# Argmax, gather and scatter-add on one core: one one-hot for both lists, a first load in two parts, and the last scatters behind the fallback branch with one-word transfers after them

## The chip, the cores and the metric

One core of a Trainium2 chip. The metric is the device time of one execution in microseconds (us). "Span" is the profiled execution, which is some 2 us shorter than its device time.

## The reference

```python
# scores (8, 2048, 2048) float32, values (8, 2048, 2560) float32, both random normal
best_j = np.argmax(scores, axis=2)                  # (8, 2048)
gathered = values[b_idx, best_j, :].copy()
out = np.zeros_like(values)
np.add.at(out, (b_idx, best_j, slice(None)), gathered)
```

Row j of batch b of the output is values[b, j] times the number of score rows whose maximum stands in column j. So the kernel counts. Rows drawn once are copied, rows drawn never are zeroed, and rows drawn several times are gathered, multiplied by their count and scattered.

## The kernel before

VectorE finds the argmax of 128 rows at a time (MAX8, FIND_INDEX8) and TensorE sums one-hots into counts. For each batch `value_steps` then issues sixteen "copies" of 128 rows with out-of-range indices for the rows that are not meant, and builds two dense lists of row numbers, one of the zero rows and one of the "many" rows. It builds them as a product of a one-hot over 128 places and the row numbers:

```python
        first = (6, NT)[b] if b < 2 else 4            # NT = 16
        for t in range(first):
            copy_once(t)                              # GpSimd: indirect DMA, DRAM to DRAM
        # ... rank of each row in its list, c = 0 zero rows, c = 1 many rows
        yield
        # ... lo = place mod 128, hi = place // 128, for both lists
        oh = ohp.tile([P, 2 * NT, P], FP16)
        nc.vector.tensor_tensor(
            out=oh[:], in0=lo[:].unsqueeze(2).to_broadcast([P, 2 * NT, P]),
            in1=fill_f[:].unsqueeze(1).to_broadcast([P, 2 * NT, P]), op=ALU.is_equal)
        # ... rm, rz: row numbers (and counts) at column hi
        for t in range(NT):
            nc.tensor.matmul(out=m_ps[:], lhsT=oh[:, NT + t, :], rhs=rm[:, t, :, :].rearrange("p a k -> p (a k)"),
                             start=(t == 0), stop=(t == NT - 1))
        for t in range(NT):
            nc.tensor.matmul(out=z_ps[:], lhsT=oh[:, t, :], rhs=rz[:, t, :], start=(t == 0), stop=(t == NT - 1))
        yield
        yield
        # ... lists to zi, mi and counts mc
        if b == 0:
            zeros()                                   # scatters of zero rows, copies in between
            # ... ten yields
            gathers()
        else:
            gathers()                                 # gather, multiply on ScalarE, copies in between
            zeros()
        for k in range(MCAP):                         # MCAP = 5
            scatter(staged[k], mi[:, k:k + 1])
```

A `yield` hands over to the counting of the next batch. The gathers go to six staging slots in turn (`stage()`), so a gather waits for the earlier scatter out of its slot. Batch 0 runs four steps of `value_steps` at once, the others step by step between row tiles of the next batch. The end:

```python
    nc.gpsimd.wait_ge(landed, 16 * n_free[0])         # copies and zero scatters have landed
    more = nc.values_load(over_i[0:1, 0:1], engines=[mybir.EngineType.Pool], min_val=0, max_val=2)
    with tc.If(more > 0):                             # a list was longer than its share; never with these inputs
        # ... the rest of each list, for any input
```

Of the kernel before, what the change touches and what calls it, by code (L numbers as in the profile page):

```python
# [36 lines left out]
def kernel(  # L37
# [117 lines left out]
    vslot = [0]  # L155

    def stage():
        v = vbig[:, vslot[0] * H:(vslot[0] + 1) * H]
        vslot[0] = (vslot[0] + 1) % NV
        return v  # L160

    def count_steps(b, cnt_ps):

        am = None
        for u in range(NT // R):
# [4 lines left out]
            else:  # L170
                s_tile = spool.tile([P, R * S], FP32, name="s_tile")[:]
            nc.sync.dma_start(
                out=s_tile, in_=scores[b, u * R * P:(u + 1) * R * P, :].rearrange("(p r) s -> p (r s)", r=R))
# [29 lines left out]
    def level_engines(rank, lo, hi):  # L203
# [54 lines left out]
        nc.vector.tensor_single_scalar(out=hi, in_=nth[:], scalar=3, op=ALU.logical_shift_right)  # L258
        lane = lev.tile([P, NT], U32)
        nc.vector.tensor_single_scalar(out=lane[:], in_=nth[:], scalar=LE - 1, op=ALU.bitwise_and)  # L260
        nc.vector.scalar_tensor_tensor(out=lo, in0=lane[:], scalar=float(NE), in1=eng[:], op0=ALU.mult, op1=ALU.add)

    def value_steps(b, cnt_ps):
# [17 lines left out]
        first = (6, NT)[b] if b < 2 else 4  # L281
# [25 lines left out]
        place = fin.tile([P, 2, NT], U32)  # L307
        nc.vector.tensor_copy(place[:], rank[:])
        lo = fin.tile([P, 2 * NT], U32)
        nc.vector.tensor_single_scalar(out=lo[:], in_=place[:].rearrange("p c t -> p (c t)"), scalar=P - 1, op=ALU.bitwise_and)  # L310
        hi = fin.tile([P, 2, NT], U32)
        nc.vector.tensor_single_scalar(out=hi[:], in_=place[:], scalar=7, op=ALU.logical_shift_right)
        if b == B - 1:
            level_engines(rank[:, 0, :], lo[:, 0:NT], hi[:, 0, :])
        oh = ohp.tile([P, 2 * NT, P], FP16)
        nc.vector.tensor_tensor(  # L316
            out=oh[:], in0=lo[:].unsqueeze(2).to_broadcast([P, 2 * NT, P]),
            in1=fill_f[:].unsqueeze(1).to_broadcast([P, 2 * NT, P]), op=ALU.is_equal)
# [4 lines left out]
        rz = fin.tile([P, NT, NT], FP16)  # L323
        nc.vector.tensor_tensor(out=rz[:], in0=ez[:], in1=row1_f[:].unsqueeze(2).to_broadcast([P, NT, NT]), op=ALU.mult)  # L324
# [4 lines left out]
        rm = fin.tile([P, NT, 2, NM], FP16)  # L329
        nc.vector.tensor_tensor(out=rm[:, :, 0, :], in0=em[:], in1=row1_f[:].unsqueeze(2).to_broadcast([P, NT, NM]), op=ALU.mult)  # L330
        nc.vector.tensor_tensor(out=rm[:, :, 1, :], in0=em[:], in1=cnt[:].unsqueeze(2).to_broadcast([P, NT, NM]), op=ALU.mult)  # L331
        m_ps = psum_f.tile([P, 2 * NM], FP32)
        z_ps = psum_f.tile([P, NT], FP32)
        for t in range(NT):
            nc.tensor.matmul(out=m_ps[:], lhsT=oh[:, NT + t, :], rhs=rm[:, t, :, :].rearrange("p a k -> p (a k)"),  # L335
                             start=(t == 0), stop=(t == NT - 1))
        for t in range(NT):
            nc.tensor.matmul(out=z_ps[:], lhsT=oh[:, t, :], rhs=rz[:, t, :], start=(t == 0), stop=(t == NT - 1))  # L338
# [6 lines left out]
        for src, dst, n in ((m_ps, mi, NM), (z_ps, zi, NT)):  # L345
            e = fin.tile([P, n], FP32, name=f"empty{n}")
            nc.vector.tensor_scalar(out=e[:], in0=src[:, 0:n], scalar1=0.0, scalar2=BIG, op0=ALU.is_equal, op1=ALU.mult)
            nc.vector.scalar_tensor_tensor(out=dst, in0=e[:], scalar=float(b * S - 1), in1=src[:, 0:n], op0=ALU.add, op1=ALU.add)
        nc.vector.tensor_copy(mc, m_ps[:, NM:2 * NM])
# [13 lines left out]
        def zeros():  # L363
            for k in range(ZLAST if b == B - 1 else ZCAP):
                scatter(zrow[:], zi[:, k:k + 1], free_running)
                if rest:
                    copy_once(rest.pop(0))


        if b == 0:  # L370
            zeros()

            for _ in range(10):
                yield
            gathers()
        else:
            gathers()
            zeros()
        for k in range(MCAP):
            scatter(staged[k], mi[:, k:k + 1])  # L380
# [3 lines left out]
    with tc.manual_schedule(engines={ET.PE, ET.DVE, ET.Activation, ET.SP}):  # L384
        pending = iter(())
        for b in range(B):
            cnt_ps = psum_c.tile([P, NT], FP32)
            for _ in count_steps(b, cnt_ps):
                next(pending, None)
            for _ in pending:  # L390
                pass
            pending = value_steps(b, cnt_ps)
            if b == 0:
                for _ in range(4):
                    next(pending)
# [12 lines left out]
    nc.gpsimd.wait_ge(landed, 16 * n_free[0])  # L408
    more = nc.values_load(over_i[0:1, 0:1], engines=[mybir.EngineType.Pool], min_val=0, max_val=2)
    with tc.If(more > 0):  # L410
        for b in range(B):
            for k in range(ZLAST if b == B - 1 else ZCAP, NT):
                scatter(zrow[:], zero_i[:, b * NT + k:b * NT + k + 1])
            for k in range(MCAP, NM):
                v = stage()
                i = b * NM + k
                gather(v, many_i[:, i:i + 1])
                nc.gpsimd.tensor_scalar(out=v, in0=v, scalar1=many_c[:, i:i + 1], scalar2=None, op0=ALU.mult)
                scatter(v, many_i[:, i:i + 1])

# [29 lines left out]
```

## Time and profile before

| | before |
|---|---|
| device time, median of 3 | 845.58 us |
| span | 843.6 us |
| VectorE busy | 696.7 us (83%) |
| DMA traffic | 347 MB |
| last landing of a scatter | 835.2 us |
| end of the span after it | 8.4 us |

What bounds the kernel is worked out in the prediction. Two lines of before, one from the timeline of VectorE (start, duration, what it waited for) and one from the page's groups of instructions (count, then busy us and mean ns of one, then idle us before them):

```profile
8.81 2.29 DVE L180 MAX8 mx<-vbig 128x8 f32<-128x2048 f32 x1 [6.45 <-DMA vbig<-in_scores_dram]
```

```profile
L316 DVE TENSOR_TENSOR oh<-lo,fill_f 128x4096 f16<-128x4096 uint32 x8 | 35.4, 4426 | 0.0
```

### The profile page before, as it was taken

What the parts mean: (1) busy time and instruction counts of PE and PEld (TensorE: products, weight loads), DVE (VectorE), ACT (ScalarE), POOL (GpSimd) and SP (SyncE); (2) the same over time, 40 slices, a digit from 0 to 9 for tenths busy, and PEclk for the clock granted to TensorE, in tenths of its full rate; (3) what the DMA queues carried; (4) which work ended last, traced back from release to release, by engine and by line L of the source; (5) the groups of instructions that cost most, each with busy time, mean ns of one, the idle gap of its engine ahead of it and who ended that gap; (6) DMA issues with size and microseconds to landing.
All of it is one profiled execution on the core that took longest, in us unless ns stands there. A gap on an engine that the chain in (4) does not pass through costs nothing.

```text
span 843.6 us, 2305 instructions
## 1 busy us (share of the span) xinstructions
PE 18.1 (2%) x401; PEld 17.0 (2%) x401; DVE 696.7 (83%) x793; ACT 103.0 (12%) x43; POOL 286.5 (34%) x277
## 2 busy tenths in 40 slices
PE   0000000000000000000000000000000000000000
PEld 0000000000000000000000000000000000000000
DVE  6999999999999999999999999999999998000000
ACT  2000000500041002210003200022000500500500
POOL 0000643137312163140263400662105725745720
DMA  9999899999999999999999999999999999999992
GB/s 376 430 428 428 308 414 420 426 395 375 426 428 427 426 428 428 426 425 427 431 425 425 428 427 427 424 429 428 426 429 420 426 424 414 422 423 423 424 417 121
DMA packets 47968, 347.05 MB, mean 411 GB/s; under 512 B 18998, under 2 KB 18998, under 8 KB 18998
## 3 DMA queue, kind: packets, MB, share of 16 engines
q0 software_dynamic: 38736, 212.67, 61.1%
q1 hardware_dynamic: 9216, 134.22, 37.6%
q14 instruction: 13, 0.11, 0.0%
q8 instruction: 3, 0.05, 0.0%
HBM read 354.42 MB, written 300.15 MB: 776 GB/s over the span
## 4 chain that ended last, share of the span: by engine, by line
DVE 68%; DMA 9%; POOL 8%; issue 6%; another core or an unknown queue 5%; PE 0%; POOLq 0%
DVE am L181 30%; DVE mx L180 28%; DMA out_dram<-vbig,many_i 8%; DVE oh L316 3%; POOL out_dram L151 3%; POOL out_dram L33 3%; DVE oh_lo L190 2%; POOL vbig L146 1%; DMA vbig<-in_scores_dram 1%; DVE lo L186 1%; DVE oh_hi L194 0%; DVE rz L324 0%; DVE ez L320 0%; DVE hi L188 0%
## 5 line engine op out<-in xcount | busy, mean ns | idle before, releaser
L181 DVE FIND_INDEX8 am<-mx,s_tile 128x8 uint32<-128x2048 f32 x116 | 265.0, 2285 | 0.0
L180 DVE MAX8 mx<-s_tile 128x8 f32<-128x2048 f32 x116 | 264.3, 2279 | 0.0
L33 POOL DMA_INDIRECT out_dram<-in_values_dram,ones_i x128 | 133.9, 1046 | 145.8 <-DVE m L287 107.7
L357 ACT ACTIVATE vbig<-vbig,many_c 128x2560 f32<-128x2560 f32 x40 | 96.8, 2427 | 697.2 <-DMA vbig<-in_values_dram,many_i 697.2
L146 POOL DMA_INDIRECT vbig<-in_values_dram,many_i x40 | 46.8, 1169 | 231.9 <-DMA out_dram<-vbig,many_i 182.1
L151 POOL DMA_INDIRECT out_dram<-vbig,many_i x40 | 44.9, 1122 | 123.1 <-ACT vbig L357 118.6
L151 POOL DMA_INDIRECT out_dram<-zrow,zero_i x61 | 59.8, 981 | 18.9 <-issue 18.3
L316 DVE TENSOR_TENSOR oh<-lo,fill_f 128x4096 f16<-128x4096 uint32 x8 | 35.4, 4426 | 0.0
L180 DVE MAX8 mx<-vbig 128x8 f32<-128x2048 f32 x12 | 27.3, 2278 | 6.5 <-DMA vbig<-in_scores_dram 6.5
L181 DVE FIND_INDEX8 am<-mx,vbig 128x8 uint32<-128x2048 f32 x12 | 27.4, 2285 | 0.0
L190 DVE TENSOR_TENSOR oh_lo<-lo,lane_f 128x512 bf16<-128x512 uint32 x32 | 22.3, 696 | 0.4
L199 PE MATMUL cnt_ps<-oh_hi,oh_lo 128*128 128x16 bf16 x128 | 8.1, 174 | 569.3 <-DVE oh_hi L194 569.3
L199 PEld LDWEIGHTS <-oh_lo 128*128 128x128 bf16 x128 | 8.4, 105 | 569.0 <-DVE oh_lo L190 567.9
L181 DVE MATCH_VALUE_LOAD am<-mx,s_tile 128x8 f32 x116 | 10.7, 92 | 4.0
L186 DVE TENSOR_SCALAR lo<-am 128x4 uint32<-128x4 uint32 x32 | 6.1, 191 | 1.1
L194 DVE TENSOR_TENSOR oh_hi<-hi,lane_f 128x64 bf16<-128x64 uint32 x32 | 6.9, 217 | 0.0
L335 PE MATMUL m_ps<-rm,oh 128*128 128x16 f16 x128 | 4.7, 175 | 88.2 <-DVE rm L331 88.2
L335 PEld LDWEIGHTS <-oh 128*128 128x128 f16 x128 | 4.1, 105 | 90.5 <-DVE rm L331 83.5
L188 DVE TENSOR_SCALAR hi<-am 128x4 uint32<-128x4 uint32 x32 | 5.7, 178 | 0.0
L338 PE MATMUL z_ps<-rz,oh 128*128 128x16 f16 x128 | 4.6, 174 | 0.0
L338 PEld LDWEIGHTS <-oh 128*128 128x128 f16 x128 | 4.0, 104 | 0.0
L324 DVE TENSOR_TENSOR rz<-ez,row_f 128x256 f16<-128x256 f16 x8 | 3.4, 424 | 0.3
(92 smaller groups left out, 65.7 us busy)
## 6 DMA issues: line engine op xcount, KB each, us to landing
s_tile<-in_scores_dram SPq DMA_DIRECT2D x58, 2048.0 KB, 12.0
vbig<-in_scores_dram SPq DMA_DIRECT2D x6, 2048.0 KB, 23.7
out_dram<-in_values_dram,ones_i POOLq DMA_INDIRECT x128, 25.6
out_dram<-zrow,zero_i POOLq DMA_INDIRECT x61, 25.8
vbig<-in_values_dram,many_i POOLq DMA_INDIRECT x40, 33.7
out_dram<-vbig,many_i POOLq DMA_INDIRECT x40, 45.4
```

The costliest lines, as they stand in the source:

```text
L33: return eng.add_instruction(ins)
L146: nc.gpsimd.indirect_dma_start(out=v, out_offset=None, in_=values_flat[:, :], in_offset=bass.IndirectOffsetOnAxis(ap=idx, axis=0), bounds_ ...
L151: note(nc.gpsimd.indirect_dma_start(out=out_flat[:, :], out_offset=bass.IndirectOffsetOnAxis(ap=idx, axis=0), in_=v, in_offset=None, bound ...
L180: nc.vector.max(out=mx[:], in_=rows)
L181: nc.vector.max_index(out=am[:, g, :], in_max=mx[:], in_values=rows)
L186: nc.vector.tensor_single_scalar(out=lo[:], in_=am[:, :, 0], scalar=P - 1, op=ALU.bitwise_and)
L190: nc.vector.tensor_tensor(out=oh_lo[:], in0=lo[:].unsqueeze(2).to_broadcast([P, G, P]), in1=lane_f[:].unsqueeze(1).to_broadcast([P, G, P]) ...
L199: nc.tensor.matmul(out=cnt_ps[:], lhsT=oh_lo[:, g, :], rhs=oh_hi[:, g, :], start=(t == 0), stop=(t == NT - 1))
L316: nc.vector.tensor_tensor(out=oh[:], in0=lo[:].unsqueeze(2).to_broadcast([P, 2 * NT, P]), in1=fill_f[:].unsqueeze(1).to_broadcast([P, 2 * ...
L335: nc.tensor.matmul(out=m_ps[:], lhsT=oh[:, NT + t, :], rhs=rm[:, t, :, :].rearrange("p a k -> p (a k)"), start=(t == 0), stop=(t == NT - 1))
L338: nc.tensor.matmul(out=z_ps[:], lhsT=oh[:, t, :], rhs=rz[:, t, :], start=(t == 0), stop=(t == NT - 1))
L357: nc.scalar.activation(out=v, in_=v, func=mybir.ActivationFunctionType.Copy, bias=0.0, scale=mc[:, k:k + 1])
```

## The change

Four intents. A row is in at most one of the two lists, so one one-hot over 16 x 128 places serves both, with the row numbers of both lists side by side in one right-hand side. The first load comes in two halves, so that VectorE can start on the first. Batch 1 is treated like batch 0: six copies first instead of sixteen, its lists at once. The last five scatters go behind the fallback branch. After each of the first four of them has landed, GpSimd moves one word from SBUF to SBUF.

```diff
+            parts = R if b == u == 0 else 1
+            for r in range(parts):
+                part = slice(r * R * S // parts, (r + 1) * R * S // parts)
+                nc.sync.dma_start(out=s_tile[:, part], in_=rows_in[:, part])
 ... (level_engines cut: same quota arithmetic, now returns one place number)
-        first = (6, NT)[b] if b < 2 else 4
+        first = 6 if b < 2 else 4
 ...
-        oh = ohp.tile([P, 2 * NT, P], FP16)
+        lo = fin.tile([P, NT], U32)
+        nc.vector.tensor_tensor(out=lo[:], in0=rank[:, 0, :], in1=rank[:, 1, :], op=ALU.min)
+        nc.vector.tensor_single_scalar(out=lo[:], in_=lo[:], scalar=P - 1, op=ALU.bitwise_and)
+        oh = ohp.tile([P, NT, P], FP16)
 ... (put: columns of many rows, counts, zero rows)
+        l_ps = psum_f.tile([P, 2 * NM + NT], FP32)
         for t in range(NT):
-            nc.tensor.matmul(out=m_ps[:], lhsT=oh[:, NT + t, :], ...)
-        for t in range(NT):
-            nc.tensor.matmul(out=z_ps[:], lhsT=oh[:, t, :], rhs=rz[:, t, :], ...)
+            nc.tensor.matmul(out=l_ps[:], lhsT=oh[:, t, :], rhs=put[:, t, :], start=(t == 0), stop=(t == NT - 1))
 ...
+        if b == B - 1:
+            last_staged.extend(staged)
+            yield
+            return
         for k in range(MCAP):
             scatter(staged[k], mi[:, k:k + 1])
 ...
-            if b == 0:
+            if b < 2:
                 for _ in range(4):
                     next(pending)
 ...
-    nc.gpsimd.wait_ge(landed, 16 * n_free[0])
     more = nc.values_load(over_i[0:1, 0:1], engines=[mybir.EngineType.Pool], min_val=0, max_val=2)
     with tc.If(more > 0):
 ...
+    word = ctx.enter_context(nc.sbuf_tensor([1, 2 * MCAP], FP32))
+    for k in range(MCAP):
+        i = (B - 1) * NM + k
+        scatter(last_staged[k], many_i[:, i:i + 1])
+    d = None
+    for k in range(MCAP - 1):
+        with tc.issue_after(d.ins) if d else nullcontext():
+            nc.gpsimd.memset(last_staged[k][0:1, 0:1], 0.0)
+        nc.gpsimd.tensor_copy(word[:, 2 * k:2 * k + 1], last_staged[k][0:1, 0:1])
+        d = nc.gpsimd.dma_start(out=word[:, 2 * k + 1:2 * k + 2], in_=word[:, 2 * k:2 * k + 1])
+        d.then_inc(landed, 16)
+        tc.info.no_tile_sem_insts.add(d.ins.name)
+        n_free[0] += 1
+    nc.gpsimd.wait_ge(landed, 16 * n_free[0])
```

The memset overwrites a word of a slot that a scatter reads, so it has to wait until that scatter has landed: that is how the word is tied to the landing.

More of the change, by code (lines that the diff above doesn't have):

```diff
@@ L1 @@
 import copy
-from contextlib import ExitStack
+from contextlib import ExitStack, nullcontext
 import concourse.bass as bass
@@ L155 @@
     vslot = [0]
+    last_staged = []
     def stage():
@@ L171, in count_steps @@
                 s_tile = spool.tile([P, R * S], FP32, name="s_tile")[:]
-            nc.sync.dma_start(
-                out=s_tile, in_=scores[b, u * R * P:(u + 1) * R * P, :].rearrange("(p r) s -> p (r s)", r=R))
+            rows_in = scores[b, u * R * P:(u + 1) * R * P, :].rearrange("(p r) s -> p (r s)", r=R)
+            parts = R if b == u == 0 else 1
+            for r in range(parts):
+                part = slice(r * R * S // parts, (r + 1) * R * S // parts)
+                nc.sync.dma_start(out=s_tile[:, part], in_=rows_in[:, part])
             if u * R % G == 0:
@@ L201, in count_steps, with level_engines @@
                 yield
-    def level_engines(rank, lo, hi):
+    def level_engines(rank):
         X = mybir.AxisListType.X
@@ L257, in level_engines @@
         nc.vector.tensor_tensor(out=nth[:], in0=rank, in1=begin[:], op=ALU.subtract)
-        nc.vector.tensor_single_scalar(out=hi, in_=nth[:], scalar=3, op=ALU.logical_shift_right)
         lane = lev.tile([P, NT], U32)
-        nc.vector.tensor_single_scalar(out=lane[:], in_=nth[:], scalar=LE - 1, op=ALU.bitwise_and)
-        nc.vector.scalar_tensor_tensor(out=lo, in0=lane[:], scalar=float(NE), in1=eng[:], op0=ALU.mult, op1=ALU.add)
+        nc.vector.tensor_scalar(out=lane[:], in0=nth[:], scalar1=LE - 1, scalar2=4, op0=ALU.bitwise_and, op1=ALU.logical_shift_left)
+        nc.vector.tensor_scalar(out=nth[:], in0=nth[:], scalar1=3, scalar2=7, op0=ALU.logical_shift_right, op1=ALU.logical_shift_left)
+        nc.vector.tensor_tensor(out=rank, in0=nth[:], in1=lane[:], op=ALU.add)
+        nc.vector.tensor_tensor(out=rank, in0=rank, in1=eng[:], op=ALU.add)
     def value_steps(b, cnt_ps):
@@ L306, in value_steps @@
             nc.vector.tensor_scalar(out=rank[:, c, :], in0=base[:, c, :], scalar1=off_ps[:, c:c + 1], scalar2=None, op0=ALU.add)
-        place = fin.tile([P, 2, NT], U32)
-        nc.vector.tensor_copy(place[:], rank[:])
-        lo = fin.tile([P, 2 * NT], U32)
-        nc.vector.tensor_single_scalar(out=lo[:], in_=place[:].rearrange("p c t -> p (c t)"), scalar=P - 1, op=ALU.bitwise_and)
+        if b == B - 1:
+            level_engines(rank[:, 0, :])
         hi = fin.tile([P, 2, NT], U32)
-        nc.vector.tensor_single_scalar(out=hi[:], in_=place[:], scalar=7, op=ALU.logical_shift_right)
-        if b == B - 1:
-            level_engines(rank[:, 0, :], lo[:, 0:NT], hi[:, 0, :])
-        oh = ohp.tile([P, 2 * NT, P], FP16)
+        nc.vector.tensor_copy(hi[:], rank[:])
+        nc.vector.tensor_single_scalar(out=hi[:], in_=hi[:], scalar=7, op=ALU.logical_shift_right)
+        lo = fin.tile([P, NT], U32)
+        nc.vector.tensor_tensor(out=lo[:], in0=rank[:, 0, :], in1=rank[:, 1, :], op=ALU.min)
+        nc.vector.tensor_single_scalar(out=lo[:], in_=lo[:], scalar=P - 1, op=ALU.bitwise_and)
+        oh = ohp.tile([P, NT, P], FP16)
         nc.vector.tensor_tensor(
-            out=oh[:], in0=lo[:].unsqueeze(2).to_broadcast([P, 2 * NT, P]),
-            in1=fill_f[:].unsqueeze(1).to_broadcast([P, 2 * NT, P]), op=ALU.is_equal)
+            out=oh[:], in0=lo[:].unsqueeze(2).to_broadcast([P, NT, P]),
+            in1=fill_f[:].unsqueeze(1).to_broadcast([P, NT, P]), op=ALU.is_equal)
         ez = fin.tile([P, NT, NT], FP16)
@@ L322, in value_steps @@
             in1=lane_f[:, 0:NT].unsqueeze(1).to_broadcast([P, NT, NT]), op=ALU.is_equal)
-        rz = fin.tile([P, NT, NT], FP16)
-        nc.vector.tensor_tensor(out=rz[:], in0=ez[:], in1=row1_f[:].unsqueeze(2).to_broadcast([P, NT, NT]), op=ALU.mult)
         em = fin.tile([P, NT, NM], FP16)
@@ L328, in value_steps @@
             in1=lane_f[:, 0:NM].unsqueeze(1).to_broadcast([P, NT, NM]), op=ALU.is_equal)
-        rm = fin.tile([P, NT, 2, NM], FP16)
-        nc.vector.tensor_tensor(out=rm[:, :, 0, :], in0=em[:], in1=row1_f[:].unsqueeze(2).to_broadcast([P, NT, NM]), op=ALU.mult)
-        nc.vector.tensor_tensor(out=rm[:, :, 1, :], in0=em[:], in1=cnt[:].unsqueeze(2).to_broadcast([P, NT, NM]), op=ALU.mult)
-        m_ps = psum_f.tile([P, 2 * NM], FP32)
-        z_ps = psum_f.tile([P, NT], FP32)
+        put = fin.tile([P, NT, 2 * NM + NT], FP16)
+        nc.vector.tensor_tensor(out=put[:, :, 0:NM], in0=em[:], in1=row1_f[:].unsqueeze(2).to_broadcast([P, NT, NM]), op=ALU.mult)
+        nc.vector.tensor_tensor(out=put[:, :, NM:2 * NM], in0=em[:], in1=cnt[:].unsqueeze(2).to_broadcast([P, NT, NM]), op=ALU.mult)
+        nc.vector.tensor_tensor(out=put[:, :, 2 * NM:], in0=ez[:], in1=row1_f[:].unsqueeze(2).to_broadcast([P, NT, NT]), op=ALU.mult)
+        l_ps = psum_f.tile([P, 2 * NM + NT], FP32)
         for t in range(NT):
-            nc.tensor.matmul(out=m_ps[:], lhsT=oh[:, NT + t, :], rhs=rm[:, t, :, :].rearrange("p a k -> p (a k)"),
-                             start=(t == 0), stop=(t == NT - 1))
-        for t in range(NT):
-            nc.tensor.matmul(out=z_ps[:], lhsT=oh[:, t, :], rhs=rz[:, t, :], start=(t == 0), stop=(t == NT - 1))
+            nc.tensor.matmul(out=l_ps[:], lhsT=oh[:, t, :], rhs=put[:, t, :], start=(t == 0), stop=(t == NT - 1))
         yield
@@ L344, in value_steps @@
         zi = zero_i[:, b * NT:(b + 1) * NT]
-        for src, dst, n in ((m_ps, mi, NM), (z_ps, zi, NT)):
-            e = fin.tile([P, n], FP32, name=f"empty{n}")
-            nc.vector.tensor_scalar(out=e[:], in0=src[:, 0:n], scalar1=0.0, scalar2=BIG, op0=ALU.is_equal, op1=ALU.mult)
-            nc.vector.scalar_tensor_tensor(out=dst, in0=e[:], scalar=float(b * S - 1), in1=src[:, 0:n], op0=ALU.add, op1=ALU.add)
-        nc.vector.tensor_copy(mc, m_ps[:, NM:2 * NM])
+        e = fin.tile([P, 2 * NM + NT], FP32)
+        nc.vector.tensor_scalar(out=e[:], in0=l_ps[:], scalar1=0.0, scalar2=BIG, op0=ALU.is_equal, op1=ALU.mult)
+        for dst, x, n in ((zi, 2 * NM, NT), (mi, 0, NM)):
+            nc.vector.scalar_tensor_tensor(out=dst, in0=e[:, x:x + n], scalar=float(b * S - 1), in1=l_ps[:, x:x + n],
+                                           op0=ALU.add, op1=ALU.add)
+        nc.vector.tensor_copy(mc, l_ps[:, NM:2 * NM])
         rest = list(range(first, NT))
@@ L378, in value_steps @@
             zeros()
+        if b == B - 1:
+            last_staged.extend(staged)
+            yield
+            return
         for k in range(MCAP):
@@ L406 @@
         nc.vector.tensor_reduce(out=over_i[:], in_=over[:], op=ALU.max, axis=mybir.AxisListType.X)
-    nc.gpsimd.wait_ge(landed, 16 * n_free[0])
     more = nc.values_load(over_i[0:1, 0:1], engines=[mybir.EngineType.Pool], min_val=0, max_val=2)
     with tc.If(more > 0):
+        v = stage()
         for b in range(B):
@@ L414 @@
             for k in range(MCAP, NM):
-                v = stage()
                 i = b * NM + k
```

## The prediction

> **What bounds the kernel now.** I read the page first, its slices before its shares:
>
> ```profile
> DVE  6999999999999999999999999999999998000000
> DMA  9999899999999999999999999999999999999992
> GB/s 376 430 428 428 308 414 420 426 395 375 426 428 427 426 428 428 426 425 427 431 425 425 428 427 427 424 429 428 426 429 420 426 424 414 422 423 423 424 417 121
> ```
>
> VectorE is busy 83% of the span, and the chain that ended last is mostly its MAX8 and FIND_INDEX8. But it has nothing left to do after 716 us of 843.6, while the DMA engines stay full for 105 us more. So the kernel is bound by its 347 MB of traffic: at the rate of the good slices (429 GB/s) they take 809 us, and some 35 us of the span are stretches in which the DMA engines were short of work. A saving counts only where it fills such a stretch. I looked for them with the view that sums stretches of time (the last two columns are the DMA share and GB/s):
>
> ```profile
> 1.00:4.00 3.00, 0.00 (x0) 0.00 (x0) 1.36 (x13) 2.99 (x2) 0.78 (x3) 1.00 0.74 191
> 4.00:84.00 80.00, 0.77 (x12) 0.79 (x12) 74.57 (x61) 3.01 (x2) 0.00 (x0) 1.00 1.01 429
> 84.00:112.00 28.00, 1.45 (x38) 1.40 (x38) 26.37 (x44) 0.00 (x0) 19.06 (x16) 1.00 0.91 334
> 94.00:98.00 4.00, 1.00 (x32) 1.01 (x32) 3.13 (x12) 0.00 (x0) 3.08 (x4) 1.00 0.66 192
> 180.00:214.00 34.00, 1.49 (x38) 1.33 (x38) 33.42 (x48) 0.00 (x0) 26.47 (x23) 1.00 0.98 373
> 214.00:640.00 426.00, 11.25 (x250) 10.54 (x250) 420.52 (x460) 48.45 (x20) 123.41 (x117) 1.00 1.01 427
> 640.00:820.00 180.00, 2.18 (x47) 1.88 (x47) 72.99 (x112) 36.20 (x15) 99.35 (x98) 1.00 1.02 422
> 820.00:836.00 16.00, 0.00 (x0) 0.00 (x0) 0.00 (x0) 0.00 (x0) 0.00 (x0) 1.00 0.53 224
> 836.00:843.60 7.60, 0.00 (x0) 0.00 (x0) 0.00 (x0) 0.00 (x0) 0.00 (x0) 1.00 0.00 0
> ```
>
> Loss of a stretch = length x (1 - rate/429): the first list stage (84 to 112) 28 x (1 - 334/429) = 6.2 us; the second (180 to 214) 34 x (1 - 373/429) = 4.4; 214 to 640 2.0; 640 to 820 2.9; the ragged finish of the 16 DMA engines (820 to 836) 7.6; an empty end of 7.6. The start loses about 2.7. What happens in the first list stage stands in the timeline of GpSimd:
>
> ```profile
> 88.16 1.11 POOL L33 DMA_INDIRECT out_dram<-in_values_dram,ones_i  x1 [86.38 <-DVE m L287]
> 89.57 0.99 POOL L33 DMA_INDIRECT out_dram<-in_values_dram,ones_i  x1 [0.30 <-issue]
> 90.87 4.22 POOL L33 DMA_INDIRECT out_dram<-in_values_dram,ones_i  x1 [0.30 <-issue]
> 95.39 1.02 POOL L33 DMA_INDIRECT out_dram<-in_values_dram,ones_i  x1 [0.30 <-issue]
> ```
>
> An issue takes 1.28 us from start to start, but the third took 4.22 us and the fourth could start only at 95.4: VectorE ran the 128x4096 one-hot of line 316 from 89.8 to 94.2. By then the ten load buffers were full and waiting for VectorE, so there was nothing else to move. A copy moves only rows drawn exactly once, about 37% (1/e) of 128 rows of 10 KB, 0.48 MB; at one per 1.28 us that is 376 GB/s, under what the engines carry. The second list stage has the same illness: sixteen copies in a row (180.8 to 205.8), with one issue of 5.2 us under the one-hot. In the later batches a copy alternates with a fuller transfer and the rate is 427. The end, by its instructions (start times last):
>
> ```profile
> L445 POOLq DRAIN  x3: 40/107/6121, 836.7 to 843.4; - x3
> L410 POOLq INC_SWDGE_SEM  x1: 1340/1340/1340, 835.3 to 835.3; - x1
> ```
>
> After the last scatter's landing (835.2) GpSimd spends 1.34 us [...] where the branch's two ways join, then 6.12 us in a DRAIN, then 0.8 us remain. The branch itself (from 822.5, resuming at 826.3) already hides behind the scatters' landings.
>
> **What the Trainium skill says.** "SBUF — State Buffer", section "SBUF: two separate sides", says a VectorE operation with two SBUF inputs locks GpSimd out, if that reads SBUF, for the whole instruction, and that descriptors of GpSimd's DMAs then can't be written. The trace agrees: 4.22 us instead of 1, ending 0.9 us after the one-hot. "DMA: Bandwidth & Descriptors", section "Issuing engines are not separate DMA queues", says all issuers share the 16 engines; the steady 427 to 429 GB/s with loads and scatters mixed agrees. Its section "Anatomy of one DMA — SWDGE (gpsimd) path" gives a small transfer about 2 us; no one-word transfer is in this trace. "Runtime: NRT & Kernel Launch", section "Instruction fetch mechanics", says a taken branch out of the prefetched window stalls on a fetch: here 2.9 us between the compare (823.4) and the next instruction (826.3). I found no page on what GpSimd's 6.12 us DRAIN consists of.
>
> **The change, part by part.**
>
> *First load in two parts.* VectorE's first MAX8 waits until 8.81 us for the whole 2.1 MB. By the rows above 0.57 MB have moved by 4 us, so 2.1 MB are through at 4 + 1.53/0.429 = 7.6 us, and the landing and wait add 1.2. The first half (1.05 MB) is through at 5.1, so the start is near 6.3 us, 2.4 us earlier. VectorE takes 4.6 us a row tile and a megabyte takes 2.4 us to arrive: it never starves again, and all of batch 0 moves 2.4 us earlier. The DMA engines are saturated with loads meanwhile, so this is worth only what it fills after 84 us.
>
> *One one-hot.* 4096 becomes 2048 columns. From 512 (696 ns) and 4096 (4426 ns) the slope is 1.041 ns a column, so 2.29 us instead of 4.42, and the dense list of batch 0 is 10.1 - 2.1 - about 0.1 = 7.9 us; sixteen matmuls instead of 32 (some 2.8 us less in all on TensorE) lie beside other work. Over eight batches VectorE saves 17 us, nearly all off the path. What counts is that GpSimd is held 2.1 us less.
>
> *First list stage after both.* Copies start at 85.8 instead of 88.2; the load that was missing at 86 to 88 is issued in time; the 18 loads last until about 90.7; the third copy is through at about 90.5, not 95.1; the first zero scatter starts near 95 instead of 99.3. Adding 1.1 us a copy to the loads gives work to about 97, when zero scatters (about 108 rows, 2.6 us each) have come in. Of 6.2 us lost I expect 1.2 to stay: gain 5.0.
>
> *Batch 1 like the others.* Six copies first, the list at once, then copies alternating with gathers and zero scatters. The copy-only stretch shrinks from 25 to about 9 us, but the list now stops the counting for 8 us and so frees no load buffer. Of 4.4 us I keep 2.0: gain 2.4. The shorter one-hots of the other batches: 0.3 (the rate is already 427).
>
> *The end.* The join and its 1.34 us go ahead of the scatters. There they delay the last scatters from 801 to about 806, while the engines have older work until about 820 (five scatters, 1.1 MB each, 13 us, before the first engines run dry at 821): free. I read the one-word transfers as a way to let GpSimd tidy up after landed DMAs piece by piece, under the last scatter, instead of in the DRAIN. Estimate: DRAIN 6.1 to 2.5 us, saving 3.6; the last one-word transfer, started at the fourth scatter's landing, 0.8 us ahead of the fifth's, costs some 2 us after it. With the 1.34: gain 3.0. The ragged finish stays.
>
> Sum: 5.0 + 2.4 + 0.3 + 3.0 = 10.7. I shade it to 10, since losses tend to reappear: 845.6 - 10 = 835.6 us.
>
> **Rivals.** (a) The DRAIN is a fixed cost or is not touched by the small transfers. For it: nothing in the trace varies it. Then the end is 2 us of waiting less 1.34: a loss of 0.7 instead of a gain of 3.0, and 839.5 us. (b) Only the fifth scatter's loose end: the DRAIN falls to about 1 us and both early stages fill entirely: 831. (c) The dense list of batch 1 opens a new gap, no buffer freed for 8 us with GpSimd issuing small copies: the second stage loses 5 us instead of 4.4, and 840. Against it: the load buffer released by the early part of the list (line 306) comes sooner than now. (d) VectorE is the bound, as the chain suggests: then its 17 + 2.4 us would come off, and 826. Against it: the DMA engines at 1.01 to 1.02 from 214 to 820 and the 128 us between VectorE's last work and the end. (e) The branch's fetch meets full DMA engines and the scatters come too late for the engines that finish first; these are not the last ones, and the slack is 9 us: under 1 us.
>
> **Range and chances.** (a) and (c) together make 843 and (b) 831; neither extreme is likely, so 831 to 841. Faster by 2% means under 828.7: it would need all of both stages, the whole DRAIN and part of the ragged finish. I give that 3%. Slower by 2% has no mechanism that I see: 1%.
>
> **What would show it.** First MAX8 at about 6.3 us; line of the one-hot 8 x 2.3 us; no issue of GpSimd over 3 us at 85 to 97; GB/s of 84 to 112 above 410, and of 180 to 214 above 400; the rate from 214 to 820 unchanged; INC_SWDGE_SEM near 805; the DRAIN well below 6 us, with 5 to 6 us from the last scatter's landing to the end. It is wrong if the DRAIN stays at 6, if the dips move to other times instead of closing, or if the ragged finish grows by what the earlier stages gain.

## The result, and the profile after

| | before | after |
|---|---|---|
| device time, median of 6 | 845.49 us | 840.34 us |
| range | 845.15 to 847.15 | 840.14 to 841.88 |
| span | 843.6 | 839.0 |
| VectorE busy | 696.7 | 679.2 |
| last landing of a scatter | 835.2 | 830.1 |
| end of the span after it | 8.4 | 8.9 |

The ratio is 0.994 (95% interval 0.9927 to 0.9953): the same within 2%. A ratio is the mean time of one kernel's fast runs over that of the other's of the same rounds, so it is not quite the ratio of the medians. The gain is 5.2 us (4.6 in the two profiled executions) and not the 10 predicted. All of it lies ahead of the last landing, and behind it half a microsecond was lost.

The slices of the page after, to be read against those in the prediction:

```profile
GB/s 383 427 429 428 381 411 424 425 407 425 424 428 429 425 428 431 425 427 427 428 427 429 428 425 427 427 430 426 426 426 408 417 424 409 414 423 418 424 417 108
```

The two early dips are shallower (the fifth slice 381 instead of 308, the ninth and tenth 407 and 425 instead of 395 and 375). But from the 31st slice on there are dips: the 31st, 32nd, 34th and 35th slices have 408, 417, 409 and 414 where before had 420, 426, 414 and 422. The same in sums of stretches of the kernel after (last column GB/s):

```profile
84.00:112.00 28.00, 1.03 (x22) 0.97 (x22) 26.42 (x45) 0.00 (x0) 20.29 (x19) 1.00 1.00 389
170.00:204.00 34.00, 1.31 (x26) 1.23 (x26) 32.32 (x54) 2.43 (x1) 24.38 (x23) 1.00 1.01 413
204.00:620.00 416.00, 8.86 (x166) 8.54 (x166) 410.54 (x454) 46.02 (x19) 117.15 (x115) 1.00 1.01 427
620.00:805.00 185.00, 1.99 (x35) 1.79 (x35) 74.95 (x122) 36.19 (x15) 96.28 (x98) 1.00 1.01 417
```

and the late stretch of the kernel before:

```profile
620.00:805.00 185.00, 3.45 (x83) 3.07 (x83) 92.68 (x140) 36.20 (x15) 98.48 (x97) 1.00 1.01 422
```

With the prediction's measure (length x (1 - rate/429)) the first list stage loses 2.6 us instead of 6.2, and the second 1.3 instead of 4.4. The late stretch loses 185 x (1 - 417/429) = 5.2 instead of 3.0. So 2.2 us come back there of what was won early. That is an upper figure: 1 GB/s is 0.4 us here, and the control below, the same kernel again, has 419 GB/s there, which gives back 1.3 us.

The parts one by one. The first MAX8 and the one-hot of the kernel after, in the timeline and the groups:

```profile
6.07 2.29 DVE L185 MAX8 mx<-vbig 128x8 f32<-128x2048 f32 x1 [5.00 <-DMA vbig<-in_scores_dram]
```

```profile
L322 DVE TENSOR_TENSOR oh<-lo,fill_f 128x2048 f16<-128x2048 uint32 x8 | 18.3, 2292 | 0.3
```

VectorE starts 2.7 us earlier, and one one-hot takes 2292 ns instead of 4426. The timeline of GpSimd in the first list stage:

```profile
86.22 1.18 POOL L33 DMA_INDIRECT out_dram<-in_values_dram,ones_i  x1 [84.48 <-DVE m L293]
...
89.00 2.36 POOL L33 DMA_INDIRECT out_dram<-in_values_dram,ones_i  x1 [0.31 <-issue]
91.67 1.10 POOL L33 DMA_INDIRECT out_dram<-in_values_dram,ones_i  x1 [0.30 <-issue]
...
95.62 1.00 POOL L151 DMA_INDIRECT out_dram<-zrow,zero_i  x1 [0.30 <-issue]
```

The issue that falls under the one-hot takes 2.36 us (4.22 before), and the first zero scatter goes out at 95.6 (99.3 before). The one-hot and the start are as predicted. The third copy is through at 91.4 (expected 90.5), and the rate from 84 to 112 is 389 GB/s, under the 410 expected. Now the end, first GpSimd's work in its timeline, for the last of the four one-word rounds:

```profile
829.43 0.09 POOL L435 MEMSET vbig<- 1x1 f32 x1 [1.92 <-DMA out_dram<-vbig,many_i]
...
830.05 0.50 POOL L437 DMA_DIRECT2D word<-word  x1 [0.29 <-POOL word L436]
```

then its sequencer's instructions, by line (durations min/median/max in ns, then first and last start in us):

```profile
L467 POOLq DRAIN  x3: 46/102/6447, 831.8 to 838.7; - x3
```

```profile
L416 POOLq COMPARE_BRANCH  x1: 53/53/53, 782.4 to 782.4; - x1
L416 POOLq INC_SWDGE_SEM  x1: 1208/1208/1208, 795.2 to 795.2; - x1
```

The fallback branch and its join are indeed out of the way: the compare is at 782.4 and the join's 1.21 us at 795.2. The first of the last scatters goes out at 797.6, 1.4 us behind the last zero scatter (one issue normally follows another after 1.3). But the DRAIN is as long as ever: 6.45 us (6.12 before). It starts at 831.8, 1.7 us after the last scatter has landed at 830.1, because the wait ahead of it covers the last word as well. Of the four words the fastest landed 1.5 us after its issue, the slowest 4.5 (from the view of the tile `word`):

```profile
DMA to landing us min/median/max: 1.5/4.1/4.5
```

### The profile page after: what moved, and what is told of

The parts are those of the page before. It is cut to its first block, busy times and chain, and to the rows that moved or that the text cites. A ratio compares the mean times of both kernels' runs of the same rounds, so it can differ in the third digit from the quotient of the medians.

```text
span 839.0 us, 2067 instructions
## 1 busy us (share of the span) xinstructions
PE 14.7 (2%) x273; PEld 14.1 (2%) x273; DVE 679.2 (81%) x794; ACT 103.0 (12%) x43; POOL 276.7 (33%) x289
## 4 chain that ended last, share of the span: by engine, by line
DVE 69%; DMA 16%; POOL 5%; issue 4%; another core or an unknown queue 4%; ACT 0%; PE 0%; POOLq 0%; DVEq 0%
DVE am L186 32%; DVE mx L185 29%; DMA out_dram<-vbig,many_i 12%; DMA vbig<-in_values_dram,many_i 3%; DVE oh_lo L195 2%; POOL out_dram L33 2%; POOL out_dram L151 2%; DVE oh L322 2%; POOL vbig L146 1%; DMA vbig<-in_scores_dram 1%; DVE lo L191 1%; DVE oh_hi L199 0%; ACT vbig L360 0%; DVE put L337 0%
## 5 line engine op out<-in xcount | busy, mean ns | idle before, releaser
L33 POOL DMA_INDIRECT out_dram<-in_values_dram,ones_i x128 | 131.4, 1027 | 157.5 <-DVE m L293 119.4
L146 POOL DMA_INDIRECT vbig<-in_values_dram,many_i x40 | 42.4, 1061 | 231.8 <-DMA out_dram<-vbig,many_i 185.1
L151 POOL DMA_INDIRECT out_dram<-vbig,many_i x40 | 38.9, 972 | 121.5 <-ACT vbig L360 117.9
L322 DVE TENSOR_TENSOR oh<-lo,fill_f 128x2048 f16<-128x2048 uint32 x8 | 18.3, 2292 | 0.3
L186 DVE MATCH_VALUE_LOAD am<-mx,s_tile 128x8 f32 x116 | 10.7, 92 | 4.0
L340 PE MATMUL l_ps<-put,oh 128*128 128x32 f16 x128 | 4.7, 188 | 68.9 <-DVE put L337 68.9
L340 PEld LDWEIGHTS <-oh 128*128 128x128 f16 x128 | 4.7, 104 | 70.0 <-DVE oh L322 59.6
L327 DVE TENSOR_TENSOR ez<-hi,lane_f 128x256 f16<-128x256 uint32 x8 | 3.4, 419 | 0.0
L337 DVE TENSOR_TENSOR put<-ez,row_f 128x256 f16<-128x256 f16 x8 | 3.3, 417 | 0.0
```

What stands on the lines that cost most here:

```text
L33: return eng.add_instruction(ins)
L146: nc.gpsimd.indirect_dma_start(out=v, out_offset=None, in_=values_flat[:, :], in_offset=bass.IndirectOffsetOnAxis(ap=idx, axis=0), bounds_ ...
L151: note(nc.gpsimd.indirect_dma_start(out=out_flat[:, :], out_offset=bass.IndirectOffsetOnAxis(ap=idx, axis=0), in_=v, in_offset=None, bound ...
L186: nc.vector.max_index(out=am[:, g, :], in_max=mx[:], in_values=rows)
L322: nc.vector.tensor_tensor(out=oh[:], in0=lo[:].unsqueeze(2).to_broadcast([P, NT, P]), in1=fill_f[:].unsqueeze(1).to_broadcast([P, NT, P]), ...
L340: nc.tensor.matmul(out=l_ps[:], lhsT=oh[:, t, :], rhs=put[:, t, :], start=(t == 0), stop=(t == NT - 1))
```

## The experiments

Twelve runs on three chips, each beside runs of the kernel before on the same chip (medians 846.85, 847.54 and 847.29 us). All were correct. First the tail, then the early parts.

### The tail: which part of it costs what

**No one-word transfers.** The expectations name theories by letter. A: the DRAIN can run beside transfers under way, and the words only delay it. B: the DRAIN is a fixed 6 us behind the last landing, words or none. C: the words do shorten it.

```diff
-    d = None
-    for k in range(MCAP - 1):
-        ... (memset, copy, one-word transfer: all cut)
     nc.gpsimd.wait_ge(landed, 16 * n_free[0])
```

> The changed kernel without the one-word transfers and the memsets and copies before them; the last wait is then for the free-running copies and zero scatters alone. What the DRAIN of 6.1 us (before) and 6.4 us (after) consists of is open. Theory A, fixed work that needs nothing landed: GpSimd reaches the DRAIN at about 817 us, when the free-running transfers have landed, it is over by 824 and the end comes 0.8 us after the last scatter's landing near 830: span 831, time 832.5. Theory B, fixed work that starts only when everything has landed: DRAIN ends near 836.5, span 837.5, time 839. Theory C, work for each transfer that GpSimd has not tidied up after, which the one-word transfers shorten: the DRAIN ends later than 838, span 840 or more, time 841.5 or more.

Measured 835.33 us (834.72 to 836.56), ratio 0.9874. GpSimd's DRAIN, by line:

```profile
L458 POOLq DRAIN  x3: 40/107/15647, 816.5 to 832.7; - x3
```

It starts at 816.5, as soon as the last copies and zero scatters have landed, and ends at 832.1. The last scatter landed at 829.0. So it lies under the landings of the last scatters, except for 3.1 us, and the span ends 3.9 us after the last landing instead of 8.9. B and C fall. A had the direction, but was 2.8 us too hopeful: a part of the DRAIN stays.

**The waits of the words without the words.** The memsets remain, so GpSimd still waits for each landing.

```diff
-        ... (copy and one-word transfer cut)
+    for k in range(MCAP):
+        nc.gpsimd.memset(last_staged[k][0:1, 0:1], 0.0)
     nc.gpsimd.wait_ge(landed, 16 * n_free[0])
```

> The changed kernel with a one-word memset after each of the five last scatters' landings (so GpSimd waits for all five, as in the kernel before) but no copies and no one-word transfers. Theories A and B (the DRAIN is fixed work): it starts near 830.4 us instead of 831.75, lasts 6.1 to 6.4 us, and the span is 837.5, the time 839.0, 1.3 us under the changed kernel. Theory C (the one-word transfers tidy up): the DRAIN is longer than 7 us and the time is 840.5 or more.

Measured 838.60 us (838.10 to 839.35), ratio 0.9908. Its last memset (timeline) and its DRAIN (by line):

```profile
829.94 0.09 POOL L433 MEMSET vbig<- 1x1 f32 x1 [0.69 <-DMA out_dram<-vbig,many_i]
```

```profile
L460 POOLq DRAIN  x3: 40/113/6249, 829.9 to 836.7; - x3
```

With the last landing at 829.9 the DRAIN starts at 829.9 and takes 6.25 us again. This splits the price of the words, as the time from the last landing to the end of the span: 3.9 us with no wait, 7.1 with the waits alone, 8.9 with the words. Arriving late at the DRAIN costs 3.2, and the last word's own landing 1.8.

**Still earlier.** If starting the DRAIN before the last landing hides half of it, would starting it before anything has landed hide the rest? The final wait goes to SyncE.

```diff
     ... (e1: no words)
-    nc.gpsimd.wait_ge(landed, 16 * n_free[0])
+    nc.sync.wait_ge(landed, 16 * n_free[0])
```

> The run without one-word transfers, with the last wait (for copies and zero scatters) on the sync engine, so that GpSimd reaches its DRAIN at about 803 us instead of 816. There the DRAIN began at 816.5, took 15.6 us and ended 3.1 us after the last landing; when all had landed before it, it took 6.1 to 6.4. If the DRAIN is work that goes on beside the landings and only its last part is exposed: it ends about 3 us after the last landing again, and the time is the same 835.3 within 0.5. If an earlier start hides more: 832.5 to 834.

Measured 835.58 us (835.40 to 836.40), ratio 0.9859.

```profile
L458 POOLq DRAIN  x3: 40/113/34033, 799.7 to 834.3; - x3
```

The DRAIN begins right after the last issue and lasts 34 us, but it still ends 3.1 us after the last landing (830.7), and the span 3.9 us after it. So some 3 us follow the last landing however early it starts.

**The control and the best version, on one chip.** The kernel after against itself unchanged, and e1 again.

> The changed kernel itself again, as the control on the same chip for the three beside it. Last landing near 830 us, the end 8.9 us later (DRAIN 6.45 us, begun 1.6 us after the last landing), about 5 us faster than the kernel before in the same rounds.

> The kernel without one-word transfers again, now on one chip with the control. If the one-word transfers cost what the traces say (end 3.9 us after the last landing instead of 8.9): 5.0 us under the control, within 0.7. If the earlier comparison was one of chips: less than 3 us under it.

Measured 840.83 us (840.33 to 841.25), ratio 0.9921, for the kernel after: 6.5 us under the kernel before on that chip, where about 5 were expected. Without the words 835.09 us (834.45 to 836.95), ratio 0.9861: 5.7 us less, just outside the 5.0 within 0.7 that was expected, and 12.2 less than the kernel before on that chip (847.29). In the profiles the stretch behind the last landing is 5.0 us shorter, and the landing itself came 1.1 us earlier (828.8 against 829.9). The DRAINs, of the control and of the version without words:

```profile
L467 POOLq DRAIN  x3: 46/102/6447, 831.5 to 838.4; - x3
```

```profile
L458 POOLq DRAIN  x3: 40/107/15657, 816.2 to 832.4; - x3
```

This version beats both kernels.

**The tail alone, on the kernel before.** All early parts undone, the last scatters behind the branch, no words.

```diff
     ... (kernel before, up to here)
+        if b == B - 1:
+            last_staged.extend(staged)
+            yield
+            return
 ...
-    nc.gpsimd.wait_ge(landed, 16 * n_free[0])
     ... (values_load, branch)
+    for k in range(MCAP):
+        i = (B - 1) * NM + k
+        scatter(last_staged[k], many_i[:, i:i + 1])
+    nc.gpsimd.wait_ge(landed, 16 * n_free[0])
```

> The kernel before with only this of the change: the last scatters follow the branch, the wait for copies and zero scatters comes last, no one-word transfers. If the end is worth what the traces say and independent of the early stages: last landing as in the kernel before (835.2, at most 1 us apart), the DRAIN begun before it and over 3 us after it, time 4.5 us under the kernel before. If moving the scatters behind the branch starves the DMA engines: last landing 2 us or more later. Had the one-word transfers or the early stages been needed for the gain at the end: within 1 us of the kernel before.

Measured 842.37 us (841.63 to 843.69), ratio 0.9943: 4.9 us under the kernel before. Its DRAIN and its stretches:

```profile
L453 POOLq DRAIN  x3: 40/107/15679, 823.3 to 839.6; - x3
```

```profile
84.00:112.00 28.00, 1.45 (x38) 1.40 (x38) 24.36 (x43) 0.00 (x0) 18.87 (x16) 1.00 0.92 338
165.00:215.00 50.00, 1.75 (x42) 1.59 (x42) 49.22 (x62) 2.43 (x1) 27.63 (x24) 1.00 0.98 384
620.00:805.00 185.00, 3.44 (x83) 3.06 (x83) 95.05 (x142) 36.20 (x15) 97.55 (x96) 1.00 1.01 423
```

The last landing is at 836.0, where before's profile has it at 835.2, and the end 3.9 us behind it instead of 8.4. The tail without words is thus worth 4.5 to 4.9 us by itself. Against this run the control shows the early parts by themselves: the last landing comes at 829.9 instead of 836.0, 6.1 us earlier (5.1 between the first two profiles).

### The early parts

**Each part undone**, with the rest of the change, words and all, in place. First the split load:

```diff
-            parts = R if b == u == 0 else 1
+            parts = 1
```

> The changed kernel with the first load in one piece again. The first MAX8 goes from 6.1 back to about 8.8 us; the counts of batch 0 were ready only 2.0 us earlier with the split (85.1 against 87.1), since constants of 0.8 us moved behind the first MAX8. Theory M (a hole in the mean DMA rate is time lost): copies start 2.0 us later and the hole of batch 0 grows by about 1.9 us; time 842.2. Theory S (only the DMA engine that lands last counts): the same here, since that hole stops all 16 engines alike; last landing 1.5 to 2 us later. If neither holds, no change: 840.3.

Measured 842.26 us (842.14 to 842.92), ratio 0.9941. Both theories had 842.2. The first MAX8 is back at 8.62, the first copy goes out at 87.99, the first list stage loses 28 x (1 - 365/429) = 4.2 us instead of 2.6:

```profile
84.00:112.00 28.00, 1.04 (x22) 0.98 (x22) 26.03 (x46) 0.00 (x0) 18.84 (x18) 1.00 0.95 365
```

**Batch 1 as before:**

```diff
-        first = 6 if b < 2 else 4
+        first = (6, NT)[b] if b < 2 else 4
 ...
-            if b < 2:
+            if b == 0:
                 for _ in range(4):
```

> The changed kernel with batch 1 as before (its 16 copies in a row, its list spread over the counting of batch 2). Theory M: the second stage loses 3.0 us more of mean DMA rate, so the time is 843.3. Theory S: in the changed kernel the last landing of batch 1's scatters came only 4.3 us earlier than before, of which 3.6 were there already at batch 0's, so the slowest engine gained about 0.8 us in this stage, and the time is 841.1; the spread between first and last landing after 280 us falls from 30 to about 20 us, as before the change, and the dips after 620 us close.

Measured 842.98 us (841.35 to 843.39), ratio 0.9941.

```profile
165.00:215.00 50.00, 1.31 (x26) 1.24 (x26) 49.20 (x65) 0.87 (x1) 29.61 (x29) 1.00 1.00 392
620.00:805.00 185.00, 2.00 (x35) 1.80 (x35) 74.03 (x122) 36.20 (x15) 95.40 (x97) 1.00 1.01 419
```

The second stage loses 50 x (1 - 392/429) = 4.3 us, against 1.2 in the kernel after over the same stretch (419 GB/s). The late stretch doesn't recover: 4.3. The spread that theory S in the expectation names (the time between the first and the last of the 16 engines' landings of one transfer) was 31 us for the fourth gather of batch 2 and not 20: that detail of S failed, and the time lies by M's 843.3 and not by S's 841.1.

**The one-hot issued twice,** which gives VectorE its old work back, and more:

```diff
         nc.vector.tensor_tensor(out=oh[:], ..., op=ALU.is_equal)
+        nc.vector.tensor_tensor(out=oh[:], ..., op=ALU.is_equal)      # the same again
```

> The changed kernel with the one-hot of 2048 columns computed twice, so that VectorE holds GpSimd and the list takes as long as with two lists. If holding GpSimd in the first two batches is what the halved one-hot was worth: an issue of over 4 us near 88 to 92, the first zero scatter of batch 0 2.2 us later, and a time of 841.8 to 842.5. If VectorE's work itself counted, eight times 2.29 us, it would be 858. If the hole of batch 0 was closed by the split load alone: 840.3.

Measured 843.48 us (840.79 to 843.65), ratio 0.9944.

```profile
84.00:112.00 28.00, 1.04 (x22) 0.98 (x22) 26.10 (x44) 0.00 (x0) 20.37 (x18) 1.00 0.97 372
165.00:215.00 50.00, 1.31 (x26) 1.24 (x26) 47.81 (x63) 6.29 (x4) 32.32 (x30) 1.00 1.00 407
```

The first stage loses 3.7 us, the second 2.6. Parts of the expectation failed: instead of one issue over 4 us there were two, of 2.37 and 2.02 us, the first zero scatter came 1.0 us later (96.66) and not 2.2, and the time is above the range. The eight extra one-hots are 18 us of VectorE, and the loads end at 634.4 instead of 619.3, but the time rises by under 3 us. VectorE's work as such doesn't count; only where it holds up GpSimd and the lists.

By medians the three cost 1.4, 2.2 and 2.7 us against the control's 840.83. That comparison crosses chips. The kernel without words speaks for it, since its medians agree within 0.5 us on all three chips (835.33; 835.58 with the wait on SyncE; 835.09). Against it, the ratios to before (0.9941, 0.9941 and 0.9944) differ by only 0.002 from the control's 0.9921, with intervals that overlap, and hardly at all from the 0.9940 of the first result. So each part may be worth some 1 to 3 us by itself, but that is not shown beyond noise, and their order isn't settled. What is shown is the three together, 6.1 us on the last landing.

**Are the loads the filler that the late stretch lacks?** In the kernel after VectorE gets through the scores sooner, so the loads end at 619.3 (634.9 before), just where the late dips begin. One theory (G in the text) was that the later waits used to be filled by these loads. An idle MAX8 in the lists of batches 2 to 7 slows VectorE, without touching the early stages:

```diff
+        if b >= 2:
+            idle = small.tile([P, 8], FP32, name="idle")
+            nc.vector.max(out=idle[:], in_=zrow[:, 0:S])
```

> The changed kernel with one useless MAX8 over 2048 columns (2.28 us, one input) in the list of batches 2 to 7, which gives VectorE back the 2.1 us a batch that the halved one-hot saved there, without holding GpSimd. Theory G (given back): the loads end 12 us earlier than in the kernel before, and then nothing fills the DMA engines while GpSimd waits for a staging slot; slower lists move the end of the loads from 620 to about 632 us, the dips near 635 to 655 and 695 to 720 us close, and the time falls by 1.5 to 2.5 us to about 838.3 in spite of 14 us more work on VectorE. Rival H (the dips come from engines that hold unequal numbers of rows, whenever the loads end): no change, 840.3 within 0.5. Rival V (VectorE matters at the end): slower, 842 or more.

Measured 840.57 us (839.89 to 841.83), ratio 0.9928. The loads ended at 629.7, and the late stretch stayed as it was:

```profile
620.00:805.00 185.00, 2.57 (x51) 2.36 (x51) 88.94 (x135) 36.20 (x15) 98.61 (x98) 1.00 1.01 416
```

G falls. The time is the one that H named, but its reason, unequal numbers of rows, was not tested. The run also shows that 14 us more work on VectorE cost nothing.

**Zero scatters ahead of the gathers** in batches 5 and 6, to have work queued when a gather has to wait for its slot:

```diff
         if b == 0: ...
+        elif b in (5, 6):
+            zeros()
+            gathers()
         else: ...
```

> The changed kernel with the zero scatters of batches 5 and 6 ahead of their gathers, as batch 0 has it: these need no staging slot, so GpSimd puts seven more transfers (7.7 MB, 18 us) in the queue before it waits for the scatters of the batch before. Theory G: the dips after 620 us shrink to half or less, time about 838.5. Rival H: no change, 840.3 within 0.5. A loss (over 841) would say that the gathers, now later, hold up their own scatters.

Measured 852.96 us (852.61 to 854.11), ratio 1.0083, worse than both kernels.

```profile
640.00:700.00 60.00, 1.74 (x31) 1.53 (x31) 55.97 (x104) 12.14 (x5) 11.09 (x13) 1.00 0.93 384
```

The gathers go out later and so hold up their own scatters: GpSimd sat idle from 645.6 to 680.3, waiting for ScalarE's multiplications, with nothing left to issue.

**A run that told nothing of its question.** The two halves of the load let 0.8 us of VectorE's constants slip in between the first MAX8 and its FIND_INDEX8 and later ones. I tried to put them ahead by fixing their order:

```diff
     ... (e1: no words)
+    with tc.manual_schedule(engines={mybir.EngineType.DVE}):
         row_f = consts.tile([P, NT], FP32)
         ... (all constants of VectorE, unchanged)
```

> The kernel without one-word transfers, and with VectorE's constants (0.8 us) kept ahead of the first MAX8, where it only waits, instead of behind it, where the split load's earlier landing let them slip. The counts of batch 0 should be ready near 84.3 instead of 85.1 us. If the hole of batch 0 still follows VectorE: 0.5 to 0.8 us faster than the run without one-word transfers. If the slowest DMA engine gains nothing more there: the same within 0.4.

Measured 835.50 us (835.23 to 836.57), ratio 0.9862. The timeline shows that the edit didn't do what was meant, since the first constant still follows the first MAX8:

```profile
8.17 0.16 DVE L90 CAST row_f<-row_i 128x16 f32<-128x16 int32 x1
```

So it is one more repeat of e1 and says nothing of the constants. A seventh staging slot was also tried for the late dips, but it didn't fit in SBUF, so there is no run of it.

### The late dips, from the landing records

Before trusting the stretches further I counted, for single transfers, when the first and the last of the 16 DMA engines reported their share (times in us, from the trace's landing records):

| transfer | before: first, last (spread) | after: first, last (spread) |
|---|---|---|
| batch 0, fifth scatter | 177.5, 190.0 (12.5) | 173.6, 186.4 (12.8) |
| batch 1, fifth scatter | 292.7, 310.2 (17.5) | 283.4, 305.8 (22.4) |
| batch 2, fourth gather | 329.2, 354.1 (24.9) | 316.9, 353.7 (36.9) |
| a gather issued at 591.4 / 596.3 | 642.0, 656.5 (14.5) | 632.5, 652.3 (19.8) |

The early filling gave the fastest engine 9.3 us at batch 1's fifth scatter and the slowest only 4.4: the mean rate rises by more than the slowest engine gains. What a larger spread does stands in GpSimd's timeline after, where a gather waits for the scatter out of its slot, and in the stretches around it:

```profile
598.05 0.99 POOL L33 DMA_INDIRECT out_dram<-in_values_dram,ones_i  x1 [0.30 <-issue]
634.83 1.01 POOL L146 DMA_INDIRECT vbig<-in_values_dram,many_i  x1 [35.79 <-DMA out_dram<-vbig,many_i]
```

```profile
630.00:635.00 5.00, 0.00 (x0) 0.00 (x0) 4.93 (x6) 0.00 (x0) 0.17 (x1) 1.00 0.98 406
635.00:640.00 5.00, 0.00 (x0) 0.00 (x0) 4.96 (x4) 0.00 (x0) 3.65 (x4) 1.00 0.94 369
```

A slot is free when the last engine is through with it, here at 634.0. The first engine had landed its share of the gather of 596.3 at 632.5, and behind that only its share of one copy (598.05) was left. The new gather went out at 634.8, 2.3 us after that landing. Before, the wait ended at 639.2, 2.9 us ahead of the first engine's landing at 642.0. Over the runs the rate follows that lead:

| run | next gather issued ahead of the first engine's landing | GB/s from 630 to 640 |
|---|---|---|
| tail alone on before | 3.6 us | 421 |
| before | 2.9 | 422 |
| one-hot twice | 2.2 | 420 |
| batch 1 as before | 0.5 | 414 |
| idle MAX8 | -0.2 | 405 |
| control | -2.2 | 395 |
| after | -2.3 | 387 |

The other six runs with this order of issues have leads of -1.1 to -2.5 and 394 to 403 GB/s. Thirteen profiles show this relation, but no run moved the lead alone, so that the lead is the cause is argued and not shown. This dip is about 0.8 us of the 2.2 that came back: 10 x (422 - 387)/429. The rest lies in smaller dips near 650, 700 and 715. Which early part makes them stays open: the late loss is in every variant with any of the early parts (3.9 to 5.6 us by printed rates, although with the one-hot twice the dip at 630 is gone), and it is smaller in before and the tail alone (3.0 and 2.6).

## Why the prediction was right or wrong

The range held, by 0.7 us, and the class was right, but half of the gain was missing. By its own steps:

- **Bound by traffic, not by VectorE: right, shown.** 18 us of extra one-hots on VectorE cost under 3 us and 14 us of idle MAX8 nothing. Rival (d), 826 us, is out.
- **First load in two parts: right.** First MAX8 at 6.07 (expected 6.3). Counts were ready 2.0 us earlier rather than 2.4, since 0.8 us of constants came behind the first MAX8.
- **One-hot and dense list: right.** 2.29 us (expected 2.29), list of batch 0 7.94 us (expected 7.9), first zero scatter at 95.6 (expected near 95).
- **The two early stages: holes right, worth too large.** Expected to be left were 1.2 and 2.0 us, measured 2.6 and 1.3: together 6.7 recovered of the 7.4 expected. But the last landing moved by only 5.1 (6.1 on the second pair). The step that failed is to take a recovered mean-rate hole as time off the end: 2.2 us (1.3 in the control's profile) were lost again between 620 and 805. For 0.8 of them the landing records point to a staging slot that came free with the slowest of engines 20 us apart; the rest is open. The text's own warning, "if the dips move to other times instead of closing", came partly true. Shading 10.7 to 10 was too little.
- **The fallback branch and its join ahead of the scatters: right, and free.** The scatters were not delayed at all (797.6; a delay of 5 us to about 806 was expected), which is rival (e)'s "under 1 us".
- **"I read the one-word transfers as a way to let GpSimd tidy up after landed DMAs piece by piece": wrong, and the largest error.** The DRAIN was to fall from 6.1 to 2.5 us (a figure that no line of the profile gave) and the end to gain 3.0. The DRAIN stayed, at 6.45, and the end lost 0.5. This is rival (a), with its loss of 0.7 and 839.5 us: "not touched by the small transfers" holds. Its other reason, a fixed cost, does not: the DRAIN can lie under landings, and is then exposed for 3.1 us. The words prevent exactly that, since GpSimd comes to it only after everything has landed. The saving was in a piece of the change that the prediction had booked as 1.34 us: the last scatters behind the branch, with the long wait for the other transfers over before these land. Alone it is worth 4.5 to 4.9: in the profiles the 1.5 us between the last landing and the DRAIN (835.2 to 836.7 before) and 3.0 of the DRAIN itself. The words then cost 5.0 to 5.7.
- **Rival (c), a new gap in batch 1's list: out.** The second stage improved, so its 840, the figure nearest to the result, is near by luck. Nor does it follow from the prediction's own terms: 5 us lost instead of 2.0 kept takes 3.0 off a gain of 10 to 10.7, which leaves 837.9 to 838.6, and (a) and (c) together come to 841.6 to 842.3 and not 843.

What the DRAIN works on is not shown. Only that started 12.5 us or more before the last landing it ends 3.1 us after it, and that started behind it, it takes 6.1 to 6.5 us (7.0 in the run with zero scatters first).

## What to carry to other kernels

At the end of a program, let the engine that issued the DMAs reach its final drain while the last transfers are still under way. A wait per landing, or any small work tied to the last landing, puts the drain behind it, here for 3 to 5 us. And when idle stretches of DMA are counted from a mean rate, ask whether the slowest of the 16 engines gains: where buffers are reused, they come free with the slowest, and what only the fast ones gained is in part given back.

## What the Trainium skill lacked or had wrong

- "VectorE: DVE Perf Modes", section "The DRAIN you can't avoid", puts the DRAINs that the runtime adds before and after a program at about 12 ns, constant, on all five engines. SyncE's take 7 ns here, which is of that order. GpSimd's first one at the kernel's last line, which may not be of that kind, takes 6.12 us (before) and 6.45 us (after) when all its transfers have landed, and 15.6 to 34 us when they have not, ending 3.1 us after the last landing. I found no page with that.
- "DMA: Bandwidth & Descriptors", section "Anatomy of one DMA — SWDGE (gpsimd) path", gives a small transfer about 2 us. The one-word transfers took 1.5, 4.1 and 4.5 us (least, median, most) from issue to landing: the one behind empty engines is in line with the page, and those issued while scatters were under way took twice as long.
- "Runtime: NRT & Kernel Launch", section "Instruction fetch mechanics", says that a taken branch out of the prefetched window stalls on a fetch. 5.4 us lay between the compare (782.4) and the next instruction (787.8), but they delayed no DMA issue: the sequencer was that far ahead of the issues still to be carried out. That the 5.4 us are the fetch is not shown, and I found no page that says of this stall that it can be hidden so.
- I found no page with a figure for the spread of the 16 engines: the first and the last share of one transfer landed 1 us apart in the first loads, 6 to 7 us in the first gathers and 37 us at the fourth gather of batch 2 (kernel after).
